# Holding the splits of the output projection's weights behind the splits of the merged stream's transposes

## The chip, the cores and the metric

The kernel runs on one core of one Trainium2 chip. The metric is the device time of one execution in microseconds (us); lower is better, and the number that is compared is the median over several executions.

## The reference, cut to what matters

The program is a decoder trunk of two layers over 256 tokens of width 1024. In each layer three mixers (DeltaNet, windowed attention, cross-attention to a memory) work on the same stream `h`. Their outputs go through one weight each, are weighted by a sigmoid gate and added, and the sum goes through one output projection, a residual and a LayerNorm before the second SwiGLU:

```python
gates = jax.nn.sigmoid(gates.reshape(B_, S_, N_BRANCH, D))
merged = jnp.sum(gates * jnp.einsum('bsnc,ncd->bsnd', branches, w_branch), axis=2)
h = layer_norm(DEEPNORM_ALPHA * h + merged @ w_out, ln_g[1], ln_b[1])
return layer_norm(DEEPNORM_ALPHA * h + 0.5 * swiglu(h, ffn2_w_gu, ffn2_w_down), ln_g[2], ln_b[2])
```

Everything is fp32. The change touches the stretch from the last branch (branch 2) to the LayerNorm behind `merged @ w_out`, once in each layer.

## The kernel before, in words

**Precision.** A fp32 product is made of three matmuls: each operand is split into a high part in fp32r (a cast on ACT) and a low part (a subtraction on DVE). `split` does that at L121, for weights and for activations, so every weight tile costs one ACT cast and one DVE subtraction. `mm3` issues the three matmuls; the activations are the stationary operand, the weights the moving one. In the rows of a profile the moving tile stands first behind the arrow, the stationary one second: `acc<-whi,w` streams a weight's high part against an activation tile named `w`.

**Weights.** All weights lie in one DRAM stream. `unit()` (L105 on) takes the next 512 KB: a `raw` tile (pool `praw`, four buffers), a load that SP issues at L115, and the split. The halves go to the rings `whi`/`wlo` (five buffers each) or to fixed tiles given by `dst`. A `raw` buffer is free for the fourth next load once DVE has made the low half. `unit` raises its instructions' priority (`AHEAD`), so the scheduler, which fixes each engine's order when the program is built, puts a weight's split ahead of work that stands earlier in the source. With `behind`, a split is held behind a given instruction on each engine.

**The stretch.** Call the two blocks of 128 tokens tb 0 and 1 and the halves of the width q 0 and 1.

- `branch(2, oT)` makes four groups of 12 matmuls, (tb, q) = (0,0), (0,1), (1,0), (1,1). Behind each, DVE multiplies by the gate (L988) and POOL adds into `mg[tb]` (L990).
- `merge_turn(tb, q)`, called a turn here, transposes four 128x128 blocks of `mg` on PE (`transpose`, L133, rows `sm<-cs,u`), and `split` puts them into `mgT`, four tiles whose tags are `w0` to `w3` in this kernel. `mgT` is the stationary operand of the output projection.
- The output projection (`projA`) has eight weight units, W0 to W7 here, one for each 128 of the 1024 rows. W0 and W1 (the leads) go to the rings, W2 to W7 to fixed tiles. PE takes W0 and W1 for tb 0, then for tb 1, and then one accumulator after the other over W2 to W7: `acc` of tb 0 q 0, tb 0 q 1, tb 1 q 0, and two quarters of tb 1 q 1 (`at`, 256 columns each). Turns (1,0) and (1,1) come between the leads, from `between`.
- `Post` adds each finished accumulator to the residual (L409), gathers statistics, and applies the LayerNorm with two tiles `gB`, `bB` (scale and shift, broadcast over the partitions by two loads of SP, L78). The `bB` multiply-add is L287. Then `h` is transposed (`sm<-cs,h`) and split into `hT`, which the first matmuls of the second SwiGLU read (`Ffn.first`, L323 to L326). Its first four weight units are called F0 to F3 here.

Tags `u0` to `u9` lie in a pool that is placed first (`NEAR`), tags `w0` to `w3` in one that is placed later.

Of the kernel before, what the change touches and what calls it, by code (L numbers as in the profile page):

```python
# [11 lines left out]
F32R = mybir.dt.float32r  # L12
# [5 lines left out]
P = 128  # L18
# [20 lines left out]
def tile_trunk(ctx, tc, x, xT, mem, memT_, wst, lnp, memln, cvw, rows, cst, out):  # L39
# [22 lines left out]
    def T(pool, shape, tag, dt=F32, bufs=None):  # L62
        pool = pn if pool is pu and tag in NEAR else pool
        kw = {} if bufs is None else {"bufs": bufs}
        return pool.tile(shape, dt, tag=tag, name=nm(tag), **kw)
# [38 lines left out]
    def unit(w=U, dst=None, cuts=1, behind=None):  # L104
        ahead = tc.high_priority(offset=AHEAD) if pos[0] >= 8 * P * U else nullcontext()  # L105
        raw = T(praw, [P, U], "raw")
        src = wst[pos[0]:pos[0] + P * w].rearrange("(p w) -> p w", p=P)
        pos[0] += P * w
        (ph, th), (pl, tl) = dst or ((phi, "whi"), (plo, "wlo"))
        with ahead:  # L110
            hi = T(ph, [P, U], th, F32R)
            lo = T(pl, [P, U], tl, F32R)
            for i in range(cuts):
                c = slice(i * w // cuts, (i + 1) * w // cuts)
                nc.sync.dma_start(raw[:, c], src[:, c])  # L115
                with tc.issue_after(behind) if behind else nullcontext():
                    newest[:] = split(hi[:, c], lo[:, c], raw[:, c])
        return hi, lo

    def split(hi, lo, src):  # L120
        return nc.scalar.copy(hi, src).ins, nc.vector.tensor_tensor(lo, src, hi.bitcast(F32), op=ALU.subtract).ins  # L121
# [52 lines left out]
            (b,) = yield from projB_parts(xt, 2, 4)  # L174
            use(i, b)

    def projA(xt, w, kpu, nk, outs, tail=0, dsts=(), lead=0, after=None, behind=None, held=(), led=None, along=None, ends=()):

        def one(k, kk, hi, lo, tb, j):
            ts = slice(tb * P, (tb + 1) * P)  # L180
            n = [o.shape[-1] for o in outs[tb]]
            first = k == ((nu - tail) * kpu if tb and j and ends and len(outs[1]) > 2 else 0)
            c = kk * w + sum(n[:j])
            c = slice(c, c + n[j])
            mm3(outs[tb][j], (xt[0](k)[:, ts], xt[1](k)[:, ts]), (hi[:, c], lo[:, c]), first, k == nk - 1 or bool(ends and tb and j and k == (nu - tail) * kpu - 1))

        nu = nk // kpu
        units = {}

        def get(uu):  # L190
            if uu not in units:
                t = uu - (nu - tail)
                units[uu] = unit(kpu * w, dsts[t] if 0 <= t < len(dsts) else None, behind=behind if uu in held else None)
            return units[uu]

        def run(us, tb, js):
            for uu in us:
                for kk in range(kpu):
                    for j in js:
                        one(uu * kpu + kk, kk, *get(uu), tb, j)  # L200

        for tb in range(2):
            run(range(lead), tb, range(len(outs[tb])))
            if led:
                led(tb)
        for uu in range(lead, nu - tail):
            for tb in range(2):
                run([uu], tb, range(len(outs[tb])))
            if along and uu in along:
                along[uu](*newest)  # L210
        for uu in range(nu - tail, nu):
            get(uu)
        turns = ()
        if ends:
            after.early(outs[1].pop())
            outs[1] += ends
        for tb in range(2):
            for j in range(len(outs[tb])):
                run(range(nu - tail, nu), tb, [j])
                if j and turns:  # L220
                    turns.pop(0)()
            turns = after and after(tb, outs)
# [21 lines left out]
    def to_T(put, tb, src, q):  # L244

        ps = sm()
        for j in range(4):
            k = q * 4 + j
            transpose(ps[:, j * P:(j + 1) * P], src[:, k * P:(k + 1) * P], ident)
        hi, lo = put(q)  # L250
        ts = slice(tb * P, (tb + 1) * P)
        split(hi[:, :, ts], lo[:, :, ts], ps.rearrange("p (j t) -> p j t", j=4))

    def rsqrt(y, v, t):

# [258 lines left out]
    def mixers(l, hT, mkT, mv_, post):  # L514
# [509 lines left out]

        def merge_turn(tb, q):
            if not mgT:
                mgT.extend(T(pu, [P, 4, S], f"w{i}", F32R) for i in range(4))
            to_T(lambda q: (mgT[q], mgT[2 + q]), tb, mg[tb], q)

        weave(branch(2, oT), {  # L1030
            3: [lambda: merge_turn(0, 0)],
            4: [lambda: merge_turn(0, 1)]})

        def between(tb):

            merge_turn(1, tb)
            pinned[0] = tb == 0

        outs, ends = full_rows()
        projA((lambda k: mgT[k // 4][:, k % 4, :], lambda k: mgT[2 + k // 4][:, k % 4, :]), D, 1, KD, outs, 6,  # L1040
              [((pu, a), (pu, b)) for a, b in (("u6", "u7"), ("u10", "u11"), ("u12", "u13"), ("u0", "u1"), ("u2", "u3"), ("u8", "u9"))], 2, post, led=between, ends=ends)


    hT = new_hT()
# [136 lines left out]
```

## Time and profile before

| what | value |
|---|---|
| median of 3 runs | 1279.35 us (1277.74 to 1280.58) |
| the profiled execution's own time | 1280.75 us |
| span of the profile | 1279.0 us |
| PE busy | 1263.0 us, 99% |
| DVE, ACT, POOL busy | 866.5, 660.6, 210.6 us |
| TensorE's granted clock, mean | 0.998 |

The span runs from the first to the last instruction; 1.75 us of the execution's own time lie outside it. PE's busy share counts a matmul from its start to its modelled end, and consecutive matmuls overlap, so a small loss on PE shows in the distance between starts rather than in the busy share.

### The profile page before, as it was taken

How to read it: one execution, taken by the hardware profiler on the slowest of the kernel's cores; microseconds unless marked ns; L12 is line 12 of the kernel's file. 1: busy time of each engine (PE TensorE's matmuls, PEld its weight loads, DVE VectorE, ACT ScalarE, POOL GpSimd, SP SyncE). 2: the span in 40 equal slices, each digit the busy share in tenths (PEclk: the TensorE clock that was granted, in tenths of full speed). 3: DMA queues.
4: the chain of work that ended last, by engine and by line, in shares of the span. 5: the costliest groups of instructions: out<-in, count | busy, mean ns of one | idle time of the engine just before them, and what ended most of it. 6: DMA issues, size and time to landing. Idle time of an engine off the chain costs nothing.

```text
span 1279.0 us, 18765 instructions
## 1 busy us (share of the span) xinstructions
PE 1263.0 (99%) x6948; PEld 1073.8 (84%) x6948; DVE 866.5 (68%) x1271; ACT 660.6 (52%) x980; POOL 210.6 (16%) x365
## 2 busy tenths in 40 slices
PE   9999999999999999999999999999999999999997
PEld 6888889999878788888888888899987787888886
DVE  5788576886647776665776665759767388766655
ACT  6556444655664534444354554456656654444441
POOL 0232100002311202221012220010033102122200
PEclk9999999999999999999999999999999999999999
DMA  8988764655534728776667876556463256577762
GB/s 285 315 269 278 254 210 161 206 176 129 170 116 148 259 97 265 244 239 220 224 204 243 256 253 223 173 187 209 152 163 136 97 191 221 167 246 244 237 225 82
DMA packets 77499, 261.40 MB, mean 204 GB/s; under 512 B 11904, under 2 KB 13056, under 8 KB 77408
## 3 DMA queue, kind: packets, MB, share of 16 engines
q1 hardware_dynamic: 66320, 232.53, 55.2%
q0 software_dynamic: 11088, 27.68, 8.0%
q8 instruction: 54, 0.88, 0.3%
q14 instruction: 37, 0.30, 0.1%
HBM read 246.40 MB, written 13.76 MB: 203 GB/s over the span
## 4 chain that ended last, share of the span: by engine, by line
PE 89%; DMA 4%; DVE 3%; issue 2%; POOL 1%; ACT 1%; SPq 0%; DVEq 0%; ACTq 0%; POOLq 0%
PE acc L130 79%; PE at L130 3%; PE sm L130 3%; DMA raw<-in_wst_dram 2%; DVE wlo L121 2%; PE sm L133 1%; DMA w<-dr 1%; PE acc L323 1%; PE acc L324 1%; PE acc L326 1%; ACT whi L121 1%; PE at L133 1%; POOL t L797 1%; POOL l L788 0%; POOL t L798 0%
## 5 line engine op out<-in xcount | busy, mean ns | idle before, releaser
L121 DVE TENSOR_TENSOR wlo<-raw,whi 128x1024 fp32r<-128x1024 f32 (+2 forms) x403 | 489.3, 1222 | 282.1 <-ACT whi L121 280.2
L121 ACT CAST whi<-raw 128x1024 fp32r<-128x1024 f32 (+2 forms) x403 | 413.4, 1033 | 401.8 <-PE acc L130 321.4
L130 PE MATMUL acc<-whi,hT 128*128 128x512 f32 (+1 forms) x1824 | 563.2, 386 | 0.7 <-ACT whi L121 0.6
L130 PEld LDWEIGHTS acc<-whi,hT 128*128 128x128 f32 x1824 | 340.5, 188 | 70.3 <-ACT whi L121 3.0
L130 PE MATMUL acc<-wlo,hT 128*128 128x512 f32 (+1 forms) x912 | 350.7, 385 | 0.8 <-DVE wlo L121 0.8
L130 PE MATMUL acc<-whi,u 128*128 128x512 f32 x784 | 249.0, 392 | 0.0
L130 PEld LDWEIGHTS acc<-wlo,hT 128*128 128x128 f32 x912 | 171.6, 188 | 33.8 <-DVE wlo L121 1.7
L130 PEld LDWEIGHTS acc<-whi,u 128*128 128x128 f32 x784 | 147.3, 188 | 30.6
L130 PE MATMUL acc<-wlo,u 128*128 128x512 f32 x392 | 152.8, 390 | 0.0
L353 POOL DMA_DIRECT2D tr<-t x176 | 96.2, 553 | 304.3 <-DVE t L347 295.1
L130 PE MATMUL acc<-hT,whi 128*128 128x256 f32 x672 | 122.3, 284 | 0.0
L130 PEld LDWEIGHTS acc<-hT,whi 128*128 128x128 f32 x672 | 104.7, 192 | 0.0
L130 PE MATMUL acc<-hT,wlo 128*128 128x256 f32 x336 | 95.2, 283 | 0.0
L130 PEld LDWEIGHTS acc<-wlo,u 128*128 128x128 f32 x392 | 73.7, 188 | 14.7
L130 PEld LDWEIGHTS acc<-hT,wlo 128*128 128x128 f32 x336 | 64.4, 192 | 0.0
L354 POOL DMA_DIRECT2D pt<-tr x44 | 25.0, 568 | 194.7 <-DMA tr<-t 148.5
L344 ACT ACTIVATE t<-acc 128x256 f32<-128x256 f32 x88 | 33.5, 380 | 38.3 <-PE acc L130 38.2
L990 POOL TENSOR_TENSOR u<-u,gt 128x512 f32<-128x512 f32 x16 | 24.4, 1529 | 131.0 <-DVE gt L988 131.0
L345 DVE TENSOR_TENSOR t<-t,acc 128x256 f32<-128x256 f32 x88 | 36.7, 417 | 9.1 <-ACT t L344 4.7
L121 DVE TENSOR_TENSOR u<-pt,u 128x512 fp32r<-128x512 f32 x44 | 28.9, 657 | 11.8 <-ACT u L121 11.8
L121 DVE TENSOR_TENSOR u<-raw,u 128x1024 fp32r<-128x1024 f32 x24 | 30.9, 1290 | 7.4 <-ACT u L121 7.4
L130 PE MATMUL acc<-whi,w 128*128 128x512 f32 x96 | 31.8, 402 | 3.6 <-DVE w L121 3.5
(236 smaller groups left out, 1204.3 us busy)
## 6 DMA issues: line engine op xcount, KB each, us to landing
raw<-in_wst_dram SPq DMA_DIRECT2D x409, 512.0 KB, 4.4
tr<-t POOLq DMA_DIRECT2D x176, 64.0 KB, 3.8
pt<-tr POOLq DMA_DIRECT2D x44, 256.0 KB, 5.0
raw<-in_wst_dram SPq DMA_DIRECT2D x16, 324.0 KB, 2.9
gB<-in_lnp_dram SPq DMA_DIRECT2D x6, 512.0 KB, 5.9
bB<-in_lnp_dram SPq DMA_DIRECT2D x6, 512.0 KB, 5.9
w<-dr POOLq DMA_DIRECT2D x4, 512.0 KB, 11.5
t<-in_xT_dram SPq DMA_DIRECT2D x4, 256.0 KB, 6.1
```

Of the source, the lines that this page charges most:

```text
L121: return nc.scalar.copy(hi, src).ins, nc.vector.tensor_tensor(lo, src, hi.bitcast(F32), op=ALU.subtract).ins
L130: return pe(nc.tensor.matmul(*a, **k))
L133: return pe(nc.tensor.transpose(*a))
L323: nc.tensor.matmul(ps, hT[0][:, k, ts], hi[:, c], start=k == 0, stop=False)
L324: nc.tensor.matmul(ps, hT[0][:, k, ts], lo[:, c], start=False, stop=False)
L326: nc.tensor.matmul(ps, hT[1][:, k, ts], hi[:, c], start=False, stop=k == KD - 1)
L344: act = nc.scalar.activation(t[:, :, tb, :], g, AF.Silu).ins
L345: ins = nc.vector.tensor_tensor(t[:, :, tb, :], t[:, :, tb, :], u, op=ALU.mult).ins
L353: nc.gpsimd.dma_start(d[:, :, q].rearrange("b c x -> c b x"), z[32 * q:32 * q + 32].rearrange("c (b x) -> c b x", b=4))
L354: back = nc.gpsimd.dma_start(y, d.rearrange("b c q x -> (b c) (q x)")).ins
L797: nc.gpsimd.tensor_tensor(pr16[:, :, 0:n], ab[j // 8][:, j % 8, :, j + 1:16], y16[:, :, j:j + 1].to_broadcast([P, 8, n]), op=ALU.mult)
L990: nc.gpsimd.tensor_tensor(mg[tb][:, js], mg[tb][:, js], gt[tb][:, js], op=ALU.add)
```

## The change

The weights of the output projection are no longer all made by `projA`. A list `wo` is filled by `fetch`, one unit at a time: one behind each of the four steps of branch 2, and one behind each of the four steps of the leads. A unit that is fetched after a turn gets that turn's two split instructions as `behind`, so its cast and its subtraction stand behind them on ACT and on DVE. `mgT` moves to the tags `u0` to `u3`, and W6 and W7 go to `w0` to `w3`. `between` is now called after each lead, and PE's order in the leads is held for longer.

```diff
@@ -113,7 +113,9 @@
-                with tc.issue_after(behind) if behind else nullcontext():
+                with ExitStack() as held:
+                    for b in behind if isinstance(behind, tuple) else (behind,) if behind else ():
+                        held.enter_context(tc.issue_after(b))
                     newest[:] = split(hi[:, c], lo[:, c], raw[:, c])
@@ -185,7 +187,7 @@
-        units = {}
+        units = units or {}
@@ -200,9 +202,10 @@
         for tb in range(2):
-            run(range(lead), tb, range(len(outs[tb])))
-            if led:
-                led(tb)
+            for uu in range(lead):
+                run([uu], tb, range(len(outs[tb])))
+                if led:
+                    led(tb, uu)
@@ -1024,21 +1027,32 @@
         def merge_turn(tb, q):
             if not mgT:
-                mgT.extend(T(pu, [P, 4, S], f"w{i}", F32R) for i in range(4))
-            to_T(lambda q: (mgT[q], mgT[2 + q]), tb, mg[tb], q)
+                mgT.extend(T(pu, [P, 4, S], f"u{i}", F32R) for i in range(4))
+            turned[:] = to_T(lambda q: (mgT[q], mgT[2 + q]), tb, mg[tb], q)
+
+
+        homes = [((pu, a), (pu, b)) for a, b in (("u6", "u7"), ("u10", "u11"), ("u12", "u13"), ("u8", "u9"), ("w0", "w1"), ("w2", "w3"))]
+        wo, turned = {}, []
+
+        def fetch():
+            n = len(wo)
+            wo[n] = unit(dst=homes[n - 2] if n > 1 else None, behind=tuple(turned))
 
         weave(branch(2, oT), {
-            3: [lambda: merge_turn(0, 0)],
-            4: [lambda: merge_turn(0, 1)]})
-
-        def between(tb):
-
-            merge_turn(1, tb)
-            pinned[0] = tb == 0
+            1: [fetch],
+            2: [fetch],
+            3: [lambda: merge_turn(0, 0), fetch],
+            4: [lambda: merge_turn(0, 1), fetch]})
+
+        def between(tb, uu):
+
+            if uu == 0:
+                merge_turn(1, tb)
+            fetch()
+            pinned[0] = not (tb and uu)
 
         outs, ends = full_rows()
-        projA((lambda k: mgT[k // 4][:, k % 4, :], lambda k: mgT[2 + k // 4][:, k % 4, :]), D, 1, KD, outs, 6,
-              [((pu, a), (pu, b)) for a, b in (("u6", "u7"), ("u10", "u11"), ("u12", "u13"), ("u0", "u1"), ("u2", "u3"), ("u8", "u9"))], 2, post, led=between, ends=ends)
+        projA((lambda k: mgT[k // 4][:, k % 4, :], lambda k: mgT[2 + k // 4][:, k % 4, :]), D, 1, KD, outs, 6, (), 2, post, led=between, ends=ends, units=wo)
```

The diff alone does not show the engines' new order. The rows below are those of layer 0, and layer 1 reads alike. Numbers behind a name tell buffers apart.

On DVE before, around turns (0,0) and (0,1): `w2_753<-sm_755` and `w3_754<-sm_757` are the two turns' low halves, `gt` the gates' products, `u..<-raw` and `wlo..<-raw` the weights' low halves.

```order
L988 SCALAR_TENSOR_TENSOR gt_686_3940<-gt_686_3940,acc_749_4217 128x512
L121 TENSOR_TENSOR u13_780_4350<-raw_778_4348,u12_779_4349 128x1024
L121 TENSOR_TENSOR u1_783_4356<-raw_781_4354,u0_782_4355 128x1024
L988 SCALAR_TENSOR_TENSOR gt_687_3941<-gt_687_3941,acc_750_4232 128x512
L121 TENSOR_TENSOR u3_786_4362<-raw_784_4360,u2_785_4361 128x1024
L121 TENSOR_TENSOR w2_753_4249<-sm_755_4251,w0_751_4247 128x4x128
L121 TENSOR_TENSOR wlo_769_4300<-raw_767_4298,whi_768_4299 128x1024
L121 TENSOR_TENSOR u9_789_4368<-raw_787_4366,u8_788_4367 128x1024
L988 SCALAR_TENSOR_TENSOR gt_687_3941<-gt_687_3941,acc_756_4258 128x512
L121 TENSOR_TENSOR w3_754_4250<-sm_757_4273,w1_752_4248 128x4x128
```

On DVE after the change, the same place and on to turn (1,0), `u2_759<-sm_776`:

```order
L991 SCALAR_TENSOR_TENSOR gt_686_3940<-gt_686_3940,acc_752_4223 128x512
L991 SCALAR_TENSOR_TENSOR gt_687_3941<-gt_687_3941,acc_756_4244 128x512
L123 TENSOR_TENSOR u2_759_4261<-sm_761_4263,u0_757_4259 128x4x128
L123 TENSOR_TENSOR u7_764_4272<-raw_762_4270,u6_763_4271 128x1024
L123 TENSOR_TENSOR wlo_755_4240<-raw_753_4238,whi_754_4239 128x1024
L991 SCALAR_TENSOR_TENSOR gt_687_3941<-gt_687_3941,acc_765_4276 128x512
L123 TENSOR_TENSOR u3_760_4262<-sm_766_4291,u1_758_4260 128x4x128
L123 TENSOR_TENSOR u11_769_4300<-raw_767_4298,u10_768_4299 128x1024
L123 TENSOR_TENSOR u2_759_4261<-sm_776_4316,u0_757_4259 128x4x128
L123 TENSOR_TENSOR u13_779_4325<-raw_777_4323,u12_778_4324 128x1024
```

Before, five weights (W2 to W6) had their low halves made ahead of turn (0,0)'s; now turn (0,0) stands ahead of W2, and W2, W1 and W3 stand between the first three turns.

On DVE after the change, where the accumulators of tb 0 are taken up: `h0<-acc_770` is the first residual add (L412, L409 before), the `wlo` rows are F0 to F3.

```order
L123 TENSOR_TENSOR w3_789_4368<-raw_787_4366,w2_788_4367 128x1024
L412 SCALAR_TENSOR_TENSOR h0_218<-acc_770_4304,h0_218 128x512
L123 TENSOR_TENSOR wlo_808_4539<-raw_806_4537,whi_807_4538 128x1024
L275 BN_STATS bnst_794_4416<-h0_218 128x6
L123 TENSOR_TENSOR wlo_811_4545<-raw_809_4543,whi_810_4544 128x1024
L123 TENSOR_TENSOR wlo_814_4551<-raw_812_4549,whi_813_4550 128x1024
L412 SCALAR_TENSOR_TENSOR h0_218<-acc_771_4305,h0_218 128x512
L123 TENSOR_TENSOR wlo_817_4557<-raw_815_4555,whi_816_4556 128x1024
```

Before, all four stood ahead of that add (F3, `wlo_817`, two rows ahead of it); now all four stand behind it. On SP the load of `bB` stands behind four loads that wait for the `raw` buffers of F0 to F3, before and after.

On PE the end of the projection before, where `at_763` is the last quarter (its 18 matmuls are cut here to the first and the last) and `sm_798`, `sm_799` are the transposes of `h`, tb 0:

```order
L133 MATMUL sm_798_4470<-cs_90,h0_218 128x128 x4
L130 MATMUL at_763_4285<-u6_773_4337,w0_751_4247 128x256
...
L130 MATMUL at_763_4285<-u8_788_4367,w3_754_4250 128x256
L133 MATMUL sm_799_4495<-cs_90,h0_218 128x128 x4
L323 MATMUL acc_818_4561<-whi_807_4538,hT_793_4415 128x512
```

On PE after the change, the same place:

```order
L132 MATMUL at_775_4309<-w3_789_4368,u1_758_4260 128x256
L132 MATMUL at_775_4309<-w2_788_4367,u3_760_4262 128x256
L135 MATMUL sm_798_4470<-cs_90,h0_218 128x128 x4
L135 MATMUL sm_799_4495<-cs_90,h0_218 128x128 x4
L326 MATMUL acc_818_4561<-whi_807_4538,hT_793_4415 128x512
```

The last quarter stood between the two groups of transposes; now both groups stand behind it, with nothing between them and the first matmul of the SwiGLU.

## Rows read from the trace of the kernel before

**Rows 1.** The page: busy us of each engine, share of the span, instructions.

```profile
PE 1263.0 (99%) x6948; PEld 1073.8 (84%) x6948; DVE 866.5 (68%) x1271; ACT 660.6 (52%) x980; POOL 210.6 (16%) x365
```

**Rows 2.** PE's waits, whole span: us in total, times, longest.

```profile
PE acc L130 <- DVE w L121: 3.5, 4, 1.1
```

**Rows 3.** Timeline of PE, layer 0: start, us, what, [idle before].

```profile
426.58 0.60 PE L133 MATMUL sm<-cs,u 128*128 128x128 f32 x4
...
429.79 0.60 PE L133 MATMUL sm<-cs,u 128*128 128x128 f32 x4
430.50 0.50 PE L130 MATMUL acc<-whi,w 128*128 128x512 f32 x1
430.84 0.40 PE L130 MATMUL acc<-wlo,w 128*128 128x512 f32 x1
432.35 0.73 PE L130 MATMUL acc<-whi,w 128*128 128x512 f32 x2 [1.12 <-DVE w L121]
...
433.15 0.63 PE L130 MATMUL acc<-whi,w 128*128 128x512 f32 x2
433.97 0.50 PE L130 MATMUL acc<-wlo,w 128*128 128x512 f32 x1 [0.19 <-DVE wlo L121]
...
437.09 1.08 PE L130 MATMUL acc<-u,w 128*128 128x512 f32 x4
438.84 0.73 PE L130 MATMUL acc<-whi,w 128*128 128x512 f32 x2 [0.67 <-DVE w L121]
```

**Rows 4.** Timeline of PE, layer 1, the same place.

```profile
1062.27 0.60 PE L133 MATMUL sm<-cs,u 128*128 128x128 f32 x4
1062.77 0.50 PE L130 MATMUL acc<-whi,w 128*128 128x512 f32 x1
```

**Rows 5.** Timeline of ACT, layer 0, around turn (0,0).

```profile
428.92 1.05 ACT L121 CAST u<-raw 128x1024 fp32r<-128x1024 f32 x1 [0.22 <-DMA raw<-in_wst_dram]
429.88 0.58 ACT L121 CAST w<-sm 128x512 fp32r<-128x512 f32 x1
```

**Rows 6.** Timeline of DVE, then of POOL, the same place.

```profile
430.48 1.22 DVE L121 TENSOR_TENSOR u<-raw,u 128x1024 fp32r<-128x1024 f32 x1
431.61 0.69 DVE L121 TENSOR_TENSOR w<-sm,w 128x512 fp32r<-128x512 f32 x1
432.21 1.71 DVE L121 TENSOR_TENSOR wlo<-raw,whi 128x1024 fp32r<-128x1024 f32 x1
...
430.64 2.20 POOL L990 TENSOR_TENSOR u<-u,gt 128x512 f32<-128x512 f32 x1 [2.75 <-DVE gt L988]
```

**Rows 7.** PE's groups over the span: busy us, mean ns, idle before.

```profile
L130 PE MATMUL acc<-u,u 128*128 128x512 f32 x108 | 26.6, 391 | 0.0
L130 PE MATMUL acc<-u,w 128*128 128x512 f32 x108 | 26.4, 398 | 0.0
```

**Rows 8.** Weight loads of SP from 405 to 445 us, and W7's alone.

```profile
DMA to landing us min/median/max: 3.5/4.4/6.0
...
DMA to landing us min/median/max: 3.8/3.8/3.8
```

**Rows 9.** Timelines of DVE (F3's low half) and SP, layer 0, and `bB`'s load.

```profile
442.08 1.22 DVE L121 TENSOR_TENSOR wlo<-raw,whi 128x1024 fp32r<-128x1024 f32 x1
...
443.71 0.42 SPq L78 DMA_DIRECT2D bB<-in_lnp_dram  x1
...
DMA to landing us min/median/max: 5.4/5.4/5.4
```

**Rows 10.** Timelines of PE and ACT at the projection's end, layer 0.

```profile
454.55 0.60 PE L133 MATMUL sm<-cs,h 128*128 128x128 f32 x4
454.90 2.36 PE L130 MATMUL at<-u,w 128*128 128x256 f32 x18
457.10 0.60 PE L133 MATMUL sm<-cs,h 128*128 128x128 f32 x4
...
455.18 0.59 ACT L121 CAST hT<-sm 128x512 fp32r<-128x512 f32 x1 [4.75 <-PE sm L133]
```

More of the change, by code (lines that the diff above doesn't have):

```diff
@@ L175, in halves, with projA @@
             use(i, b)
-    def projA(xt, w, kpu, nk, outs, tail=0, dsts=(), lead=0, after=None, behind=None, held=(), led=None, along=None, ends=()):
+    def projA(xt, w, kpu, nk, outs, tail=0, dsts=(), lead=0, after=None, behind=None, held=(), led=None, along=None, ends=(), units=None):
         def one(k, kk, hi, lo, tb, j):
@@ L251, in to_T @@
         ts = slice(tb * P, (tb + 1) * P)
-        split(hi[:, :, ts], lo[:, :, ts], ps.rearrange("p (j t) -> p j t", j=4))
+        return split(hi[:, :, ts], lo[:, :, ts], ps.rearrange("p (j t) -> p j t", j=4))
     def rsqrt(y, v, t):
```

## The prediction

> **What bounds the kernel now.** The page comes first: PE is busy for 1263.0 us, 99% of the span [rows 1], so the end moves only with time that PE loses. The view of waits, kept to PE, then names the places: the longest entry is the output projection's matmuls waiting for DVE's low half of a tile `w`, 3.5 us in four waits [rows 2]. Tile `w` is `mgT`, the transposed merged stream. The timeline of PE shows two of the four in layer 0, at 432.35 and 438.84 us [rows 3], and layer 1 repeats them. The reader should measure the loss from start to start, since an overlapped matmul hides part of it. A 512-column matmul follows the last after 0.23 us, and after four transposes PE goes on 0.35 us after their start (454.55 to 454.90) [rows 10].
>
> By that measure layer 0 loses this much [rows 3]. Behind turn (0,1), 430.50 - 429.79 - 0.35 = 0.36 us. At the first wait, 432.35 - 430.84 - 0.23 = 1.28. At W1's low half, 433.97 - 433.15 - 2 x 0.235 = 0.35. At the second wait, 438.84 - 437.09 - 4 x 0.233 = 0.82. After a pause the first matmul takes 0.34 until the next instead of 0.23 (430.50 to 430.84), which makes 0.1 for each of the three real pauses. Together **3.1 us**. In layer 1 the first item is 1062.77 - 1062.27 - 0.35 = 0.15 [rows 4], so I take 2.9.
>
> Why the low half is late stands in the timelines of ACT and DVE. Turn (0,0)'s transposes end at 427.18 [rows 3], but ACT casts them at 429.88, behind a weight whose load it had waited for [rows 5], and DVE subtracts at 431.61, behind another weight [rows 6]. Both engines run strictly in order; nothing is late but the order.
>
> **What the change removes.** The turns' splits go ahead of the weights, as the instruction order shows. Turn (0,0)'s cast can start at 427.21 and its low half be ready at 428.5 (0.59 and 0.69 us [rows 6, 10]); PE needs it at about 430.6. The first three items go, W1's low half too, since W1 is now done by 431.1. The last item is turn (1,0), and that one stays in part, below.
>
> The low homes are the other gain. The profile has the same 512-column matmul at 391 ns with a stationary tile in `u` and 398 ns with one in `w` [rows 7]. With 78 such matmuls in the projection of a layer, 7 ns each is 0.5 us of PE time. This is weighed against the Trainium skill's page "SBUF — State Buffer", section "Who interferes with whom": PE has read ports of its own and never waits on another engine, and the page knows no dependence on the address. By it these 0.5 us are nothing; by the row they are there. As it turns out below, a wait at the projection's end takes back nearly all of it, so they count only in a rival.
>
> **What the change adds: turn (1,0).** I follow DVE's new order in layer 0 with the rows' durations (a weight's low half 1.22 us, 1.13 from start to start; a turn's 0.69; POOL's add 1.1 to 1.3 once it runs). W2's cast ends at 428.74 and its low half at 430.0, W1's at 431.1, then the gate's product of the last group until 431.7. POOL's add then runs from 431.8 to 433.1. Now look at what POOL does to DVE: the subtraction at 432.21 took 1.71 us instead of 1.22, and POOL's add at 430.64 took 2.20, ending 1.14 behind the subtraction that began at 430.48; the 1.71 in turn ends 1.08 behind that add [rows 6]. The two wait for each other. A turn's subtraction at 431.61, which reads PSUM, was not slowed. So turn (0,1)'s low half is done at 432.3, but W3's, which the change puts ahead of turn (1,0), waits for POOL and ends at 434.2; turn (1,0)'s ends at 434.8. PE, no longer held, gets to that matmul at 434.34: turn (0,1) at 429.79, 0.35, six matmuls of W0 with a restart (1.46), turn (1,0) 0.35, six of W1 (1.46), four more (0.91). It waits 0.46 and restarts for 0.1: **0.56 us lost**. Behind the waiting matmul stand turn (1,1) and all of the rest.
>
> **The weights' loads.** W7's load now starts only when W3's low half frees a buffer, at 434.2; in the trace W4's low half freed it at 426.8. It lands 3.8 us later by its own row, where the loads around it range from 3.5 to 6.0 [rows 8]. At 3.8 it is there at 438.0, cast at 439.0 and subtracted at 440.8, behind W6; PE, after 24 more matmuls and turn (1,1), wants that low half at 440.8. So nothing is lost at 3.8, 0.15 us at 4.4, and about a microsecond at 5.2.
>
> **What the change adds: `bB`.** The first accumulator is complete at 441.4. DVE now adds it to the residual ahead of F0 to F3, and goes on without a gap through add, F0, statistics, F1, F2, second add, F3: 0.6 + 1.13 + 0.7 + 1.13 + 1.13 + 0.7 from 441.5, so F3's low half runs from about 446.9 to 448.2. In the trace it started at 442.08 [rows 9]. SP frees the next `raw` buffer with it, and `bB`'s load stands behind that on SP: issued at 448.55, against 443.71 now, and landing 5.4 us later [rows 9], at 453.95. Its reader, the LayerNorm's last multiply-add, would be ready near 453.2 and PE is through with the projection at 453.7 (two accumulators of 18 matmuls, 4.1 us each, and two quarters, 2.1 each [rows 10]). With `bB` there at 453.95 and 0.7 us for a half, the transposes of `h` start at 454.73: 1.0 us lost. The second half comes 0.67 later, while PE could go on after 0.35: 0.3 lost. And the first matmul of the SwiGLU needs ACT's cast, which now nothing covers: transposes take 0.60 and the cast 0.59 (454.55, 455.18 [rows 10]), so PE starts 0.23 us later than it could. Before, the last quarter stood in between. Together **1.5 us lost**. The transposes of `h` for tb 1, 20 matmuls later, find their input ready with 0.3 us to spare.
>
> The Trainium skill speaks on this too, "DMA: Bandwidth & Descriptors", section "Anatomy of one DMA — SWDGE (gpsimd) path": about 2 us fixed plus the bytes at 436 GB/s, which for 512 KB is an estimate of 3.2 us. The row says 5.4 for this load, in company of others, and I take the row. By the page `bB` would be there at 451.8 and not be waited for; that is the first rival.
>
> **The sum.** Layer 0: 3.1 - 0.56 - 1.5 + 0.5 = 1.5 us gained; layer 1, 1.3. The 0.5 brings PE to the projection's end earlier and lengthens its wait for `bB` there, which stands in the 1.5; without it both would be smaller by about as much. Together 2.8 us: 1280.75 becomes 1277.95, and the median, 1.4 below the profiled execution, 1279.35 becomes **1276.5**.
>
> **Rivals.**
> - *`bB` lands in time.* If it takes no more than 4.6 us (the weight loads' median is 4.4 [rows 8]), the first 1.0 us of that loss shrinks to 0.2: 0.8 more in each layer, 4.4 in all, 1274.9. Against it stands its own row of 5.4. If the low homes also gave nothing, this would be 1.0 less, 1275.9.
> - *Late weights.* W6, W7 and F0 to F3 are now loaded when they are nearly due. At 5.2 us for W7, PE loses another 0.95 in front of the first accumulator's end, of which the wait for `bB` gives a little back: 0.8 gained in layer 0 and 0.55 in layer 1, 1278.0.
> - *The other side: slower.* The same place at the longest load of the trace, 6.0 us [rows 8]. W7 lands at 440.2, is cast at 441.25 and subtracted at 442.5; PE waits 0.7 and 0.9 us, everything behind slides by 1.7, and with `bB` at 5.9 layer 0 is 0.7 us slower than now, layer 1 0.9: 1281.0. It decides from about 5.6 us on. For it: the trace has a 6.0 among these very loads. Against it: W7 goes out with one weight and `gB` in flight beside it, as in the trace, where it took 3.8.
>
> **How the numbers follow.** The forecast's case (1.5 to 3.7 us gained) has 0.50, `bB` in time 0.17, late weights (0.5 lost to 1.5 gained) 0.23, slower 0.10. What a measurement of this kernel tells from no change is about 0.2%, 2.6 us. Of the first case two thirds lie beyond it, 0.32, and all of the second: faster 0.49. Of the last case half lies beyond: slower 0.05. The rest, 0.46, is within. The range from 1274.4 to 1279.4 leaves out less than 0.1 on either side.
>
> **What would show it.** In the changed profile PE's waits for the turns' low halves at W0 should be gone, and one of about 0.5 us be left at turn (1,0), with W3's subtraction stretched beside POOL's add. At the projection's end DVE's last multiply-add should wait for `bB`, and PE for `h`, for about 1.5 us in each layer. No wait at W7 means its load took under 4.2 us. The forecast is wrong if `bB` is not waited for, or if PE stops in front of W6 or W7.

## The result and the profile after

The changed kernel takes 1282.76 us (median of 22 runs, 1279.81 to 1287.18), the kernel before 1279.63 us beside it (22 runs). The ratio is 1.0026, 95% interval 1.0017 to 1.0034: **3.1 us slower**, where 2.8 us of gain were forecast. The profiled execution took 1284.01 us, with a span of 1281.9 us.

The page and the view of PE's waits of the changed kernel (the waits: us in total, times, longest):

```profile
PE 1263.8 (99%) x6948; PEld 1074.6 (84%) x6948; DVE 863.2 (67%) x1271; ACT 660.5 (52%) x980; POOL 206.6 (16%) x365
```

```profile
PE sm L135 <- DVE h L290: 5.0, 3, 3.1
...
PE acc L132 <- DVE u L123: 0.8, 2, 0.4
```

The 3.5 us for the turns' low halves [rows 2] are down to 0.8. A new entry stands on top: the transposes of `h` wait 5.0 us for the LayerNorm's last multiply-add, 1.5 and 3.1 us of it at the projection's end in layers 0 and 1, and 0.4 us behind the second SwiGLU of layer 0.

The timeline of PE in the leads of layer 0, after:

```profile
426.16 0.60 PE L135 MATMUL sm<-cs,u 128*128 128x128 f32 x4
...
429.38 0.60 PE L135 MATMUL sm<-cs,u 128*128 128x128 f32 x4
429.73 0.48 PE L132 MATMUL acc<-whi,u 128*128 128x512 f32 x1
...
434.50 0.73 PE L132 MATMUL acc<-whi,u 128*128 128x512 f32 x2 [0.39 <-DVE u L123]
...
440.97 0.74 PE L132 MATMUL acc<-w,u 128*128 128x512 f32 x2 [0.20 <-DVE w L123]
```

W0 follows turn (0,1) after 0.35 us, without a wait. What is left is 0.39 us at turn (1,0) and 0.20 at W7. The timelines of POOL and DVE around turn (1,0) show why, as forecast: W3's subtraction takes 2.00 us, beside POOL's add.

```profile
431.47 1.29 POOL L993 TENSOR_TENSOR u<-u,gt 128x512 f32<-128x512 f32 x1 [2.98 <-DVE gt L991]
...
431.84 2.00 DVE L123 TENSOR_TENSOR u<-raw,u 128x1024 fp32r<-128x1024 f32 x1
433.77 0.68 DVE L123 TENSOR_TENSOR u<-sm,u 128x512 fp32r<-128x512 f32 x1
```

Now the projection's end. First layer 0: the timelines of SP, DVE and PE, and the landing of that `bB` load (the view of transfers, KB each and us to landing):

```profile
448.57 0.42 SPq L78 DMA_DIRECT2D bB<-in_lnp_dram  x1
...
454.87 1.41 DVE L290 SCALAR_TENSOR_TENSOR h<-h,rstd,bB 128x512 f32<-128x512 f32 x2 [1.76 <-DMA bB<-in_lnp_dram]
...
455.76 1.29 PE L135 MATMUL sm<-cs,h 128*128 128x128 f32 x8 [1.47 <-DVE h L290]
457.07 0.51 PE L326 MATMUL acc<-whi,hT 128*128 128x512 f32 x1
...
459.04 0.40 PE L326 MATMUL acc<-whi,hT 128*128 128x512 f32 x1
```

```profile
bB<-in_lnp_dram SPq DMA_DIRECT2D x1, 512.0 KB, 6.3
```

`bB` is issued at 448.57 (forecast 448.55; counted from turn (0,0), 0.4 us later than forecast), but lands after 6.3 us and not after 5.4 [rows 9]. Then layer 1, the same views:

```profile
1080.89 1.23 DVE L123 TENSOR_TENSOR wlo<-raw,whi 128x1024 fp32r<-128x1024 f32 x1 [1.01 <-ACT whi L123]
...
1082.52 0.42 SPq L78 DMA_DIRECT2D bB<-in_lnp_dram  x1
...
1089.17 1.42 DVE L290 SCALAR_TENSOR_TENSOR h<-h,rstd,bB 128x512 f32<-128x512 f32 x2 [2.33 <-DMA bB<-in_lnp_dram]
...
1090.07 1.50 PE L135 MATMUL sm<-cs,h 128*128 128x128 f32 x8 [3.13 <-DVE h L290]
1091.38 0.79 PE L326 MATMUL acc<-whi,hT 128*128 128x512 f32 x1
1091.97 0.63 PE L327 MATMUL acc<-wlo,hT 128*128 128x512 f32 x1
1092.39 0.63 PE L326 MATMUL acc<-whi,hT 128*128 128x512 f32 x1
...
1094.73 0.39 PE L326 MATMUL acc<-whi,hT 128*128 128x512 f32 x1
```

```profile
bB<-in_lnp_dram SPq DMA_DIRECT2D x1, 512.0 KB, 6.6
```

Here F3's low half (`wlo` at 1080.89) waited 1.01 us for its weight, `bB` went out with it and took 6.6 us, and PE paused for 3.13 us. And then something that the forecast has no word for: the matmuls behind the pause start 0.43 us apart, not 0.23. The view by windows has the granted clock in the third column from the right (PEclk):

```profile
1087.00:1090.00 3.00, 0.00 (x0) 0.00 (x0) 0.82 (x2) 0.00 (x0) 0.00 (x0) 1.00 0.11 46
1090.00:1091.40 1.40, 1.29 (x9) 0.91 (x9) 1.37 (x4) 0.59 (x1) 0.00 (x0) 0.86 0.00 0
1091.40:1094.10 2.70, 2.70 (x7) 2.13 (x7) 2.48 (x6) 0.88 (x2) 0.00 (x0) 0.50 0.00 0
1094.10:1096.80 2.70, 2.70 (x13) 2.21 (x11) 2.60 (x7) 0.00 (x0) 0.00 (x0) 0.94 0.00 0
```

Behind the pause PE ran at 0.50, the 1.2 GHz level. Transposes and the first eight matmuls take 1094.73 - 1090.07 = 4.66 us; in layer 0, at full clock, the same takes 459.04 - 455.76 = 3.28: 1.4 us lost. Layer 0's shorter pause left the clock at 1.00.

**A measure for all kernels.** In each trace the timeline of PE gives two spans per layer: from turn (0,0)'s transposes to the first quarter (the leads and the bulk of the projection), and from there to the SwiGLU's first matmul (two quarters and the transposes of `h`). Before, in layer 0, these are 452.42 - 426.58 = 25.84 and 457.46 - 452.42 = 5.04 [rows 3, 10]; layer 1 before, and the points of the changed kernel that are not shown above:

```profile
1059.08 0.60 PE L133 MATMUL sm<-cs,u 128*128 128x128 f32 x4
...
1084.67 2.29 PE L130 MATMUL at<-u,w 128*128 128x256 f32 x18
...
1089.73 0.48 PE L323 MATMUL acc<-whi,hT 128*128 128x512 f32 x1
```

```profile
449.89 1.58 PE L132 MATMUL at<-u,u 128*128 128x256 f32 x12
...
1059.22 0.60 PE L135 MATMUL sm<-cs,u 128*128 128x128 f32 x4
...
1082.54 1.58 PE L132 MATMUL at<-u,u 128*128 128x256 f32 x12
```

What is lost behind the SwiGLU's first matmul, by a lower clock or by a wait, lies outside. The differences are taken before rounding. The experiments (E) are those below.

| kernel | layer 0 | layer 1 |
|---|---|---|
| before | 25.84, 5.04 | 25.59, 5.05 |
| order of before: E3, E9, E13 | 26.06, 26.10, 24.92; each 5.03 | 24.87, 24.90, 26.31; each 5.03 |
| E2 before, low homes | 24.98, 5.04 | 24.92, 5.03 |
| E5 before, `bB` held | 25.70, 5.09 | 24.63, 5.08 |
| after | 23.73, 7.17 | 23.32, 8.84 |
| E4 after, old homes | 23.36, 7.11 | 23.36, 7.13 |
| E14 after, other norms early | 23.33, 9.14 | 23.31, 7.04 |
| E6 after, `bB` later | 23.33, 8.65 | 23.32, 9.69 |
| E1 `bB` early | 23.33, 5.91 | 23.33, 7.11 |
| E7 the same, order of after | 23.33, 5.59 | 23.32, 6.28 |
| E10 `bB` on POOL's queue | 23.32, 5.85 | 23.34, 6.28 |
| E15 all early | 23.44, 5.59 | 23.33, 6.75 |
| E8 `bB` early, F2 and F3 behind | 23.33, 5.05 | 23.33, 5.06 |
| E11 E10, F3 behind | 23.34, 5.31 | 23.34, 5.42 |
| E12 all early, F3 behind | 23.34, 5.04 | 23.35, 5.07 |

The first span fell by 2.1 and 2.3 us with the change; the second grew by 2.1 and 3.8. With the clock's 1.4 us, that makes 2.9 us lost between these two traces, whose spans differ by 2.9 us. That this is nearly the 3.1 us of the medians is in part luck, since executions of the changed order differ: in E4's trace the spans of both layers add up to 0.6 us less than before, with no fall of the clock, and in E14's the long pause stands in layer 0.

### The profile page after: what moved, and what is told of

It is laid out like the page before. It is cut to its first block, busy times and chain, and to the rows that moved or that the text cites. A ratio compares the mean times of both kernels' runs of the same rounds, so it can differ in the third digit from the quotient of the medians.

```text
span 1281.9 us, 18763 instructions
## 1 busy us (share of the span) xinstructions
PE 1263.8 (99%) x6948; PEld 1074.6 (84%) x6948; DVE 863.2 (67%) x1271; ACT 660.5 (52%) x980; POOL 206.6 (16%) x365
## 4 chain that ended last, share of the span: by engine, by line
PE 87%; DMA 6%; DVE 3%; issue 2%; ACT 1%; POOL 0%; SPq 0%; DVEq 0%; ACTq 0%; POOLq 0%
PE acc L132 77%; PE at L132 3%; PE sm L132 3%; DMA raw<-in_wst_dram 2%; DVE wlo L123 2%; PE sm L135 2%; DMA bB<-in_lnp_dram 1%; ACT whi L123 1%; PE acc L326 1%; PE acc L327 1%; PE acc L329 1%; DMA tr<-t 1%; DMA pt<-tr 1%; PE at L135 1%; DVE u L123 0%
## 5 line engine op out<-in xcount | busy, mean ns | idle before, releaser
L132 PE MATMUL acc<-whi,u 128*128 128x512 f32 x816 | 260.8, 393 | 0.8 <-DVE u L123 0.8
L132 PEld LDWEIGHTS acc<-whi,u 128*128 128x128 f32 x816 | 153.1, 188 | 33.3 <-DVE u L123 1.6
L132 PE MATMUL acc<-wlo,u 128*128 128x512 f32 x408 | 159.1, 390 | 0.0
L132 PEld LDWEIGHTS acc<-wlo,u 128*128 128x128 f32 x408 | 76.7, 188 | 15.2
L132 PE MATMUL acc<-u,u 128*128 128x512 f32 x180 | 44.6, 392 | 0.0
L993 POOL TENSOR_TENSOR u<-u,gt 128x512 f32<-128x512 f32 x16 | 20.7, 1291 | 127.2 <-DVE gt L991 127.2
L132 PEld LDWEIGHTS acc<-u,u 128*128 128x128 f32 x180 | 33.8, 188 | 7.6
```

Source lines behind the costliest of these rows:

```text
L132: return pe(nc.tensor.matmul(*a, **k))
L993: nc.gpsimd.tensor_tensor(mg[tb][:, js], mg[tb][:, js], gt[tb][:, js], op=ALU.add)
```

## The experiments

The theory: `bB`'s late landing, and nothing in the leads, takes back the gain. The rivals: the weights and turns themselves, the homes, the transposes that lost their cover. Four groups of runs were compared with the kernel before on the same chip; its medians there were 1280.17 (E1 to E4), 1279.26 (E5 to E8), 1279.49 (E9 to E12) and 1280.74 us (E13 to E15).

**E1, `bB` early** (in the changed kernel):

```diff
             2: [fetch],
-            3: [lambda: merge_turn(0, 0), fetch],
+            3: [lambda: setattr(post, 'gb', gb(*post.aps)), lambda: merge_turn(0, 0), fetch],
...
-                self.gb = gb(*self.aps)
+                self.gb = getattr(self, 'gb', None) or gb(*self.aps)
```

> The changed kernel, with gB and bB of the second Post loaded four and more weights earlier. Theory (the late bB is the loss): DVE's last multiply-add no longer waits for bB, the pauses of 1.47 us (layer 0) and 3.13 us (layer 1) in front of the transposes of h go or shrink to under 1 us, and with the second one the seven matmuls behind it that run at half the granted clock. Layer 0 gets 1.3 us back, layer 1 1.9 to 2.9 us for the wait and 1.4 us (7 x (0.43 - 0.23)) for the clock: 4.6 to 5.6 us below the changed kernel, 1.5 to 2.5 us below the kernel before. Rival A (the loss is in the late weights and the turns of the leads): bB in time changes little, less than 1 us, and the kernel stays 2 us or more above the one before. Rival B (loads in company are slow wherever they stand): gB and bB ahead of the weights make W3 to W7 late, and PE waits there for 1 us or more.

Measured: 1279.54 us, ratio 0.9993 (0.9984 to 1.0002). The loss against before is gone, so the theory stands and rival A falls; B falls too, since the first span is 23.33. One thing moved along: the schedule has put the first transposes of `h` back among the last quarter's matmuls, so E1 gives back the lost cover as well, and E7 is there to tell the two apart. But less came back than expected, 3.8 us (3.1 + 0.6, each against before) and not 4.6 to 5.6. The timeline of PE says where the rest is, in layer 0 and layer 1:

```profile
452.45 0.63 PE L135 MATMUL sm<-cs,h 128*128 128x128 f32 x4 [0.66 <-DVE h L290]
...
1084.60 0.63 PE L135 MATMUL sm<-cs,h 128*128 128x128 f32 x4 [1.88 <-DVE h L290]
```

With `bB` long there, DVE is still late: F2's and F3's low halves wait for their loads ahead of the LayerNorm (timeline of DVE, layer 1, F3):

```profile
1077.90 1.23 DVE L123 TENSOR_TENSOR wlo<-raw,whi 128x1024 fp32r<-128x1024 f32 x1 [1.23 <-ACT whi L123]
```

**E2, the homes alone** (in the kernel before), and **E4, the old homes** (in the changed kernel). Both keep every engine's order.

```diff
-                mgT.extend(T(pu, [P, 4, S], f"w{i}", F32R) for i in range(4))
+                mgT.extend(T(pu, [P, 4, S], f"u{i}", F32R) for i in range(4))
...
-("u12", "u13"), ("u0", "u1"), ("u2", "u3"), ("u8", "u9"))]
+("u12", "u13"), ("w0", "w1"), ("w2", "w3"), ("u8", "u9"))]
```

> The kernel before, with mgT in u0 to u3 and the two weights that were there in w0 to w3; the order of all engines is that of before. The row that gave 391 ns against 398: 78 matmuls a layer at 7 ns, 0.5 us a layer, so 1.0 us less in all, and matmuls acc<-u,u at 391 ns where acc<-u,w stood. Rival (the address of the stationary tile does nothing): no change, within 0.3 us, and the same duration as before.

> The changed kernel, with the old homes (mgT in w0 to w3, W6 and W7 in u0 to u3); order of all engines as in the changed kernel. Theory (PE waits for bB at the projection's end, whenever it gets there): the 0.5 us a layer that the low homes give PE is swallowed by the wait, so the time is that of the changed kernel within 0.5 us, and the waits for h are shorter by about 0.5 us each; where the second pause becomes short enough for the granted clock to stay full, 1.4 us less. Rival (the homes are the loss): 1 us or more faster. Rival (the homes are a gain that reaches the end): 1.0 us slower.

Measured: E2 1280.34 us, 1.0004 (0.9995 to 1.0012); E4 1283.18 us, 1.0027 (1.0014 to 1.0039), which is the changed kernel's ratio. The homes do nothing that shows. The difference in duration is still there (the groups of E4):

```profile
L132 PE MATMUL acc<-u,u 128*128 128x512 f32 x108 | 26.6, 390 | 0.0
L132 PE MATMUL acc<-u,w 128*128 128x512 f32 x108 | 25.9, 396 | 0.0
```

But from start to start there is none: the first span is 23.36 us with the old homes and 23.33 with the low ones, 0.03 us where 0.5 was expected. The end of an overlapped matmul in the records is not what the next one waits for. The Trainium skill ("SBUF — State Buffer", "Who interferes with whom") says that PE never waits on another engine, and names no dependence on the address; the 0.03 us agree with it.

**E3 and E5, `bB` late in the kernel before.** E3 asked for its load behind the second statistics in the order of issue alone:

```diff
+                with tc.issue_after(ins):
+                    load(self.gb[1], self.aps[1].partition_broadcast(P))
```

> The kernel before, with bB's load held until the second statistics of LayerNorm (they end at 449.85 us in layer 0, bB was issued at 443.71): nothing else moves. Theory (a late bB by itself costs what was lost): bB lands 5.3 us later at about 455.2, the multiply-add that began at 452.17 begins there, the first transposes of h at 455.95 in place of 454.55: 1.4 us or more lost in each layer, 3 to 4 us in all, without any of the change. Rival (bB's wait is covered by the last quarter, and the loss is elsewhere): within 0.5 us of before.

Measured: 1280.02 us, 1.0000 (0.9990 to 1.0010). It tells nothing: the load went out at 447.18, 17.35 us behind turn (0,0) (before: 443.71 - 426.58 = 17.13). It serves as a second trace of the kernel before. E5 makes DVE write one column of `bB` first, so that the load really waits:

```diff
                 with tc.issue_after(ins):
+                    nc.vector.memset(self.gb[1][:, 0:1], 0.0)
                     load(self.gb[1], self.aps[1].partition_broadcast(P))
```

> The kernel before, with bB's load held for good: DVE writes one column of bB behind the second statistics of tb 0 (they end at 449.85 us in layer 0 of the trace of before), and the load has to wait for that. PE's order is that of before. Theory (a late bB by itself costs what was lost): issued at about 450.0 in place of 443.7, landed at 455.3, the last multiply-add there in place of 452.17, the first transposes of h at 456.1 in place of 454.55: 1.5 us lost in each layer, 3 us in all, and 1.4 us more in a layer where the pause lowers the granted clock. Rival (the last quarter behind these transposes covers it, the loss is in the leads): within 0.5 us of before.

Measured: 1280.41 us, 1.0004 (0.9995 to 1.0013). The expectation was wrong, and the reason is the best row of the study (SP's timeline and the landing):

```profile
451.57 0.33 SPq L78 DMA_DIRECT2D bB<-in_lnp_dram  x1
```

```profile
bB<-in_lnp_dram SPq DMA_DIRECT2D x1, 512.0 KB, 3.4
```

Counted from turn (0,0), the load went out 6.1 us later than before (451.57 - 428.34 against 443.71 - 426.58), but with no other load in flight, and landed after 3.4 us, only 4.1 us later. That much the slack held: the second span is 5.09 and not 5.04. In the changed kernel `bB` lands 6.1 and 7.8 us later by the same count, so E5 does not test a lateness of that size. It shows that the issue time alone does not settle the landing: 3.4 us with no load in flight, 5.4 in the kernel before, 6.3 and 6.6 in the changed one. By SP's issues and their landings, three weights are in flight when `bB` goes out, in both kernels; why they cost more after the change is not shown, and the landing varies between executions of the changed order (5.9 and 4.5 us in E4's trace, 7.1 and 5.8 in E14's). The Trainium skill's figure ("DMA: Bandwidth & Descriptors", "Anatomy of one DMA — SWDGE (gpsimd) path") was worked out to 3.2 us in the prediction as an estimate; its section is on DMAs from gpsimd, this load goes by SP, and alone it took 0.2 us more.

**E6, `bB` later still** (in the changed kernel; the same edit, behind the last operation on `rstd`).

> The changed kernel, with bB's load held behind the last small operation on rstd (451.78 us in layer 0, 1085.72 in layer 1) in place of 448.57 and 1082.52: the dose of the suspected cause goes up by some 3 us. Theory: bB lands 5 to 6 us later, at about 457.5 and 1091.3; the pause of PE in layer 0 grows from 1.5 to 4.1 us and there, too, the granted clock falls to half behind it (1.4 us, as in layer 1 of the changed kernel); layer 1 grows by 2.2. In all 5 to 7 us above the changed kernel, near 1289. Rival on the clock (the fall in layer 1 had nothing to do with the pause): 4.8 us and a full clock in layer 0. Rival (the place of bB is not the cause): no change from the changed kernel.

Measured: 1286.78 us (5 runs), 1.0061 (1.0048 to 1.0073), 4.4 us above the changed kernel, somewhat under the 5 to 7 expected, since `bB`, nearly alone, landed after 3.6 us. Layer 0's pause grew to 2.77 us, and now its clock fell as well (PE's timeline and windows):

```profile
456.05 1.75 PE L135 MATMUL sm<-cs,h 128*128 128x128 f32 x8 [2.77 <-DVE h L292]
457.54 0.79 PE L329 MATMUL acc<-whi,hT 128*128 128x512 f32 x1
458.13 0.63 PE L330 MATMUL acc<-wlo,hT 128*128 128x512 f32 x1
```

```profile
456.00:457.40 1.40, 1.35 (x8) 1.16 (x8) 1.29 (x3) 0.50 (x1) 0.00 (x0) 0.63 0.00 0
457.40:459.00 1.60, 1.60 (x6) 1.18 (x5) 1.24 (x2) 0.67 (x2) 0.00 (x0) 0.50 0.00 0
```

The rival on the clock falls: the same code at the same place runs at 1.00 behind 1.47 us and at 0.50 behind 2.77.

**E7, the order of the changed kernel** (E1, with the transposes of `h` held behind the last quarter):

```diff
-                if j and turns:
-                    turns.pop(0)()
+                while turns and j == len(outs[tb]) - 1:
+                    with tc.issue_after(tail_[0]):
+                        turns.pop(0)()
```

> The changed kernel with gB and bB early, as in the first experiment, and with both groups of transposes of h held behind the last quarter, as the changed kernel has them. Theory (what is left in the first experiment is the transposes' wait for DVE, 0.66 and 1.88 us, and the cover itself is worth little): with the quarter run first the waits shrink, 0.2 us faster in layer 0 and 0.9 in layer 1 than the first experiment, 1.1 in all. Rival (the uncovered transposes were a good part of the loss): 0.5 to 1.5 us slower than the first experiment.

Measured: 1280.66 us, 1.0007 (0.9998 to 1.0016). In its trace the second span is 0.3 and 0.8 us shorter than E1's, as the theory has it; behind the SwiGLU's first matmul, tb 1's transposes give 0.4 us of it back in each layer. The time is not faster, but the edit reaches further than this place: it works on every call of `projA`, and behind the second SwiGLU of layer 0 it makes PE wait 1.38 us for `hT` and 0.86 us for tb 1's `h`. There E7's trace is 2.1 us longer than E1's, which is more than the 1.8 us (0.14%) between their ratios. So at the output projection nothing is left for the lost cover, by one trace of each.

**E8, F2 and F3 behind the LayerNorm** (E1, and their subtractions on DVE behind the multiply-add of tb 0):

```diff
-        return nc.scalar.copy(hi, src).ins, nc.vector.tensor_tensor(lo, src, hi.bitcast(F32), op=ALU.subtract).ins
+        cast = nc.scalar.copy(hi, src).ins
+        with tc.issue_after(low) if low else nullcontext():
+            return cast, nc.vector.tensor_tensor(lo, src, hi.bitcast(F32), op=ALU.subtract).ins
```

> The first experiment, and in addition the low halves of F2 and F3 on DVE behind the last multiply-add of the LayerNorm of tb 0. Theory (the rest of the loss is F2's and F3's low halves, which stand ahead of the LayerNorm and wait for their loads): the multiply-add starts 1.5 to 3 us earlier, PE no longer waits in front of the transposes of h, and 0.7 us in layer 0 and 1.9 in layer 1 come back: 2.0 to 2.6 us below the first experiment, 2 to 3 us below the kernel before. Rival: the same low halves are then late for the SwiGLU, or the LayerNorm of tb 1 is late behind them, PE waits there instead, and the time is that of the first experiment or more.

Measured: 1277.91 us, 0.9993 (0.9980 to 1.0005). The wait in front of `h` is gone (5.05 and 5.06), as the theory says, and part of it returns, as the rival says: tb 1's transposes come 6.1 and 6.9 us behind the SwiGLU's first matmul, not 4.3, and the hundred PE instructions behind that matmul take 23.0 and 23.7 us, not 22.0.

**E9 and E10, `bB` on POOL's DMA queue**, in the kernel before and in the changed one:

```diff
-        load(bB, bap.partition_broadcast(P))
+        nc.gpsimd.dma_start(bB, bap.partition_broadcast(P))
```

> The kernel before, with one line changed: bB is loaded on POOL's DMA queue in place of SP's, in all six LayerNorms. The order of PE, DVE and ACT is that of before. Theory (in the kernel before bB had 3 us to spare, and the loss belongs to the change): no change, within 0.5 us of before. Rival (bB's place in SP's queue costs the kernel before as well, so that the experiments with bB early gained something that has nothing to do with the change): 1 us or more faster.

> The changed kernel with the same one line: bB on POOL's DMA queue. No weight's load moves ahead or back on SP. Theory (bB's landing is the loss): the wait of the last multiply-add for bB goes, the pauses of 1.5 and 3.1 us shrink to what DVE's own order leaves (0.7 and 1.9 us in the first experiment), the granted clock stays full: 3 us below the changed kernel and 0 to 1 us below the kernel before. Rival (the first experiment gained by the weights' other order on SP, not by bB): no change from the changed kernel. Rival (the waits at the leads are the loss): no change either.

Measured: E9 1282.66 us, 1.0019 (1.0010 to 1.0028); E10 1282.11 us, 1.0020 (1.0011 to 1.0028). Neither theory had E9 slower. Its trace loses the time at the program's start: the first `bB` goes out at 1.30 us, among the first weights (PE's timeline; the window):

```profile
9.79 0.79 PE L130 MATMUL acc<-whi,hT 128*128 128x512 f32 x1 [2.79 <-ACT whi L121]
```

```profile
10.00:15.00 5.00, 5.00 (x12) 3.59 (x13) 3.80 (x5) 3.43 (x5) 0.00 (x0) 0.50 1.04 399
```

E10 pays the same 3 us there. Against each other, E10 is 0.55 us below E9 by the medians and level with it by the ratios, and its second spans are E1's or shorter. So with `bB` off SP's queue in both kernels the change costs nothing that shows, where it cost 3.1 us; the loss belongs to `bB`, not to the weights' order on SP.

**E11 and E12.** E11 is E10 with F3's low half behind the LayerNorm; E12 is E1 with that, and with `gB` and `bB` early behind both SwiGLUs:

```diff
+        ahead_gb = {12: lambda *a, p=post: setattr(p, 'gb', gb(*p.aps))}
...
-self.units.append(unit(cuts=2 if before and q == 0 else 1))
+self.units.append(unit(cuts=2 if before and q == 0 else 1, low=low if q > 2 else None))
```

> The kernel of the tenth experiment, and DVE makes F3's low half behind the last multiply-add of the LayerNorm of tb 0. Theory (what is left is F3's low half, which waits for its load ahead of the LayerNorm): the wait in front of the first transposes of h goes (0.7 and 1.9 us); behind it the LayerNorm of tb 1 is up to 1.1 us late in each layer, since F3's low half now lies ahead of it. Net 0.5 to 2 us below the tenth experiment, 1 to 3 us below the kernel before. Rival (LayerNorm of tb 1 gives it all back): the tenth experiment's time.

> The changed kernel with gB and bB early on SP in every LayerNorm behind a SwiGLU too, and F3's low half behind, as in the eleventh. Theory: as the eleventh experiment, 1 to 3 us below the kernel before; and the wait for h behind the first SwiGLU of layer 1 (0.4 us in the changed kernel's profile) goes. Rival (the two loads ahead make the weights late): PE waits for weights in the second products, no gain over the first experiment.

Measured: E11 1281.05 us, 1.0008 (0.9999 to 1.0017), 1.1 below E10, with E9's start. E12 1277.95 us, 0.9992 (0.9981 to 1.0003). In E12's trace nothing is left of the wait in front of the SwiGLU, but tb 1's transposes wait behind its first matmul (layer 0):

```profile
451.60 0.60 PE L137 MATMUL sm<-cs,h 128*128 128x128 f32 x4
...
454.51 0.47 PE L328 MATMUL acc<-whi,hT 128*128 128x512 f32 x1
...
459.53 0.63 PE L137 MATMUL sm<-cs,h 128*128 128x128 f32 x4 [0.44 <-DVE h L292]
```

**E13 to E15** ask what the other LayerNorms' loads have to do with it: only these early in the kernel before (E13) and in the changed one (E14), and E12 without F3 behind (E15).

> The kernel before, with gB and bB of the four LayerNorms behind a SwiGLU's second product loaded ahead of the last weights on SP; the LayerNorm behind the output projection is left as it is, and PE, DVE and ACT keep their order. Theory (these loads have nothing to do with the loss, and are rarely waited for): no change, within 0.7 us of before. Rival (they are waited for in many executions, and the twelfth experiment's gain is partly theirs): 1 to 2 us faster.

> The changed kernel with the same edit: its own late bB stays. Theory: the two stretches lose what they lost, so it stays 2.5 to 3.5 us above the kernel before, and only the 0.4 us wait for h behind the first SwiGLU of layer 1 goes. Rival (part of the change's loss arose at the other LayerNorms, whose loads it shifts): 1 us or more below the changed kernel.

> The changed kernel with gB and bB early in all LayerNorms, F3's low half where the schedule puts it: the twelfth experiment without its last part. Theory (F3's low half ahead of the LayerNorm costs 0.7 and 1.9 us, of which 0.9 comes back with the later LayerNorm of tb 1): 1.0 to 2.0 us above the twelfth experiment, about the first experiment's time. Rival (F3's place does nothing): the twelfth experiment's time.

Measured: E13 1280.16 us, 0.9998 (0.9986 to 1.0009); E14 1282.28 us, 1.0016 (1.0005 to 1.0028); E15 1279.14 us, 0.9985 (0.9975 to 0.9994). The other LayerNorms' loads are worth nothing in the kernel before; in the changed one about 1 us, which is not settled, since its interval here overlaps its first. (The wait of 0.4 us that the expectations of E12 and E14 place behind layer 1's first SwiGLU is the one behind layer 0's second.) E14's trace has the long pause in layer 0 this time:

```profile
456.99 1.94 PE L135 MATMUL sm<-cs,h 128*128 128x128 f32 x8 [2.98 <-DVE h L290]
```

E15 is the only one of the fifteen whose interval lies under 1, 0.15% below the kernel before; with so many comparisons that is a weak finding. E12 and E15 can't be told apart by their times.

## Why the prediction was wrong

**The leads: right.** Turn (0,0), turn (0,1) and W1 wait no more, turn (1,0) waits 0.39 us (forecast 0.46) for the reason given, W7 0.20 in layer 0 (forecast none). The first span shrank by 2.1 and 2.3 us. The forecast, without the homes, was 3.1 and 2.9 less 0.56, so 2.5 and 2.3. In the kernel before the same span ranges from 24.63 to 26.31 between traces; one execution overstated or understated it by up to a microsecond.

**The low homes: wrong.** They were to give 0.5 us a layer by the 7 ns of [rows 7]. E2 and E4 show 0.03. The row gives the length of a record, not the distance from one start to the next. The forecast's total did not rest on them: in its sum the gain and a longer wait for `bB` cancel.

**`bB`: the right place, and the step that failed by its size.** "Together 1.5 us lost" measured 2.1 us in layer 0, and 3.8 + 1.4 us in layer 1. Three things were left out. The landing was taken from `bB`'s own row of before, 5.4 us [rows 9], and after the change it took 6.3, and 6.6 in layer 1. Layer 1 was put down as a copy of layer 0, but there F3's load was late and `bB` went out with it. And a pause of PE was priced at its length, though behind a long one the granted clock is at half. E1 and E15 undo the loss by moving `gB` and `bB` (PE's old order comes back with them, which E7 takes out again), E10 undoes it by moving `bB` alone (against E9), and E6 makes it larger.

How large the step is differs between executions. E4's trace has the changed order, and F3 late in layer 1 too, but there `bB` took 4.5 us, and PE paused for less than half as long, at full clock:

```profile
1088.52 1.29 PE L135 MATMUL sm<-cs,h 128*128 128x128 f32 x8 [1.42 <-DVE h L290]
```

That execution took 1280.72 us, the shortest of E4's twelve (median 1283.18). So the long pause, and the slow matmuls behind it, come in some executions and in either layer. The granted clock of each run on record says how often, though not where it fell: its mean is 0.997 or less in 14 of the 22 runs of the changed kernel, with a median of 1284.1 us, against 1281.5 in the other eight, and in 24 of the 124 runs of the kernel before beside the experiments.

**The rivals.** The slower case was there, with W7's load as its mechanism, and it named the wrong place: W7 cost 0.2 us. The bound of 6.0 us that it used for weights belonged to `bB` first of all. By the prediction's own sum, `bB` at 6.3 and 6.6 takes 0.9 and 1.2 us off the 2.8 and leaves 0.7 us gained; the homes take nothing more, since they cancel there. From 0.7 gained to the traces' 2.9 lost, 3.0 us lie in layer 1, with its late F3 and the clock, and 0.7 in layer 0, where the leads gained 0.4 less and the end lost 0.3 more.

**Still open.** With `bB` in time and F3 behind, the two spans of E12 are 2.5 and 2.2 us shorter than in the trace of before, but its median is 1.5 us lower. Two parts of that are on record. The six traces with the order of before average 60.9 us for both spans of both layers, not the 61.5 of this one, and E12 has 56.8: 4.1 us less. Behind the SwiGLU's first matmul E12 loses 0.5 us in each layer (the hundred PE instructions there take 22.5 us, not 22.0), so 3.1 are left. The same count gives 1.5 us for E8 (measured 1.4), 0.8 for E1 (0.6) and 1.4 for E15 (1.6). For E12 1.6 us stay open. E13 excludes the other LayerNorms as a gain of before. Executions differ elsewhere too (below), and no run separates that. Nor was it tried to bring F0 to F3 back ahead of the residual add, the order of before, in the changed kernel.

## What to carry to other kernels

When a change moves splits or casts, follow what their buffers release, to the last small load in that queue, and price that load in its new company: here 512 KB took 3.4 us alone and 4.5 to 7.1 in a train. Where work that covered a wait has moved away, give a pause of TensorE a second price, the slow matmuls behind it, and look at each layer for itself. Compare matmuls from start to start, and a stretch over several traces, before a few nanoseconds or one trace's wait go into a sum.

## What the runs showed of the hardware

- The granted clock fell to 0.50 behind pauses of PE of 2.77, 2.98 and 3.13 us, for about 3 us each time, which cost 1.4 us in the changed kernel, and behind 3.53 us (E6, layer 1) for about 7; behind 1.47 and 1.88 us at the same place it stayed at 1.00. The length of a pause alone does not decide it. In E3's trace the clock fell soon behind one pause of 1.51 us, while 64 matmuls of 32x32 ran (the windows, layer 0's mixers; the 1.51 us missing from PE's 5 in the first are that pause), and over 3 us were lost there, in code that no kernel here changes:

```profile
340.00:345.00 5.00, 3.49 (x18) 2.29 (x16) 5.00 (x6) 1.52 (x2) 0.00 (x0) 1.00 0.68 195
345.00:350.00 5.00, 5.00 (x74) 3.92 (x71) 3.31 (x7) 2.64 (x9) 0.00 (x0) 0.62 0.84 274
```

  In E13's trace, with the order of before, it fell in layer 1's leads, behind waits of 1.34 and 0.20 us (PE's timeline; the window). That is the 26.31 of the table:

```profile
1065.24 0.72 PE L130 MATMUL acc<-whi,w 128*128 128x512 f32 x2 [1.34 <-DVE w L121]
```

```profile
1067.00:1069.50 2.50, 2.50 (x8) 1.98 (x9) 2.50 (x4) 1.44 (x3) 0.82 (x1) 0.54 0.71 274
```

- At the program's start one more load of 512 KB among the first weights, landing at 8.9 us, cost 3 us of the whole: PE's thirty-first instruction starts at 17.5 us (E9), 17.0 (E10) and 16.8 (E11), in the kernel before at 14.3, and in no other trace later than 15.8.
